# Up projection: operands of two products and the weight tiles of one begin at many byte residues

## The chip, the core and the metric

One core of one Trainium2 chip. The metric is device microseconds of one execution; the kernel before has a median of 1459.01 us in 3 runs (1456.24 to 1460.63). TensorE (PE) multiplies, with the weight load as a stream of its own (PEld), VectorE (DVE), ScalarE (ACT) and GpSimd (POOL) do the elementwise work, SyncE (SP) and ACT issue most DMAs.

## The reference

One layer of a hybrid decoder on 1024 tokens of width 1024: a mixing stage, then the gated MLP below, then an embedding gate and a final norm. All is fp32. The change is in the up projection of the MLP.

```python
def conv_glu_ffn(hn, w_up, conv_w, conv_b, w_down):
    u = hn @ w_up                       # (1024, 1024) @ (1024, 5632)
    up = jnp.pad(u, ((0, 0), (CONV_W - 1, 0), (0, 0)))
    uc = conv_b + conv_w[0] * up[:, 0:S_]
    for j in range(1, CONV_W):
        uc = uc + conv_w[j] * up[:, j:j + S_]
    gate, val = jnp.split(uc, 2, axis=-1)
    return (jax.nn.silu(gate) * val) @ w_down

    h = h + conv_glu_ffn(rmsnorm(h, norm_ffn_g[l]), ffn_up[l], ffn_conv_w[l], ffn_conv_b[l], ffn_down[l])
```

## The kernel before

**Precision.** Every fp32 product is made of three matmuls of type float32r: an operand is split into a part `hi` (ACT copies it to float32r) and a part `lo` (the rest, subtracted on DVE or POOL), and hi x hi, lo x hi and hi x lo are added in PSUM. In `mul` (L1388) part 0 is the weights' hi with the moving hi, part 1 the weights' hi with the moving lo, part 2 the weights' lo with the moving hi.

**Units.** The up projection (`phase_up`, L1494) runs in 22 units `f`. A unit takes 128 gate columns and 128 value columns of `ffn_up`, each loaded by SP as a 512 KB tile `raw` (four buffers, so two units). The 2 x 2 x 2 block product of a unit (gate and value columns; first and second 512 rows of the weights; first and second 512 tokens) is done with seven products instead of eight. Product n has a weight block made of sums of the raw blocks (`sums`, L1506, on DVE: `s7` is a11 + a21, `s6` adds a22, later a12) and a moving operand `TX["p1"]` to `TX["p7"]`, which is made once for all units. Each moving operand has four tiles of 128 x 512 for hi and four for lo. A product is 12 matmuls of 128 x 512 columns, a unit 84. The products run in this order, the first pairs interleaved matmul by matmul: p3 (of the unit before) with p1; p6 with p4 (of the unit before); p5 with p2; p7. Accumulators are PSUM tiles `bg` (gate half) and `bv` (value half), two of each.

**Weight tiles.** `split2` (L102) makes hi (`whi`, ACT) and lo (`wlo`) of a weight block. All seven blocks of a unit take their tiles from one ring of six buffers each, in the order 3, 1, 4, 6, 5, 2, 7; block 7's lo is made on DVE, the others' on POOL. The moving tiles of p1, p2 lie at the top of SBUF (`t16`), those of p5, p6 in tiles of the earlier stage, and those of p3, p7, p4 in a pool `ty` (`op_tiles`, L1407, filled by `op_split`). Every one of these tiles, moving or weight, begins 64 bytes past a multiple of 128 in its partition.

**Work around the products.** DVE adds the products' parts (L1564, L1572, L1576, L1585, L1587) and does the convolution (L1597, L1598) after a first pass on ACT (L1596); ACT applies silu (L1600), DVE multiplies the halves (L1605) and forms sums for the down projection (L1617 to L1620), which SP stores. L1587 reads `bv`, to which the next unit's p4 is added. In this stage the order on each engine is made by the framework's scheduler from the written order, the buffers and their releases.

Of the kernel before, what the change touches and what calls it, by code (L numbers as in the profile page):

```python
# [10 lines left out]
F32 = mybir.dt.float32  # L11
F32R = mybir.dt.float32r
U8 = mybir.dt.uint8
AF = mybir.ActivationFunctionType
ALU = mybir.AluOpType
# [3 lines left out]
P = 128  # L19
T = 1024  # L20
HT = 512
# [58 lines left out]
class Trunk:  # L80
# [1210 lines left out]
    def phase_out(self, hp, x0, emb):  # L1291


        nc = self.nc
        self.h = [hp.tile([P, T], F32, name=f"h{k}") for k in range(ND)]
        self.hd = [[self.zpool.tile([P, HT], F32, tag=f"hd{k}_{hf}", name=f"hd{k}_{hf}") for hf in (0, 1)] for k in range(ND)]
        todo = [lambda k=k: nc.scalar.dma_start(self.h[k], self.a["xT"][k]) for k in range(ND)]
        for _ in range(3):
            todo.pop(0)()
        acc = hp.tile([P, HT], F32, name="acc")  # L1300

        def rows(m, halves, hooks={}):
            w = self.load_w(self.a["w_out"][m])
            ps = self.dps.tile([P, T], F32, tag="dp", name=self.nm("dp"))
            self.dense([ps[:, :HT], ps[:, HT:]], w, self.O, (6, 7, 0, 1, 4, 2, 3, 5), halves, hooks)
            for g in halves:
                u = self.h[m][:, g * HT:(g + 1) * HT]
                nc.vector.tensor_tensor(u, u, ps[:, g * HT:(g + 1) * HT], ALU.add)
                last = nc.scalar.dma_start(self.hd[m][g], u)
            if todo:  # L1310
                with self.tc.issue_after(last.ins):
                    todo.pop(0)()

        for m in range(ND):
            rows(m, (0, 1) if m < 2 else (0,))
            self.sq_acc(acc, self.h[m][:, :HT], m == 0)
        r = {}

        def factor(i):
            if i == 0:  # L1320
                r[0] = self.rstd_sums(acc, 1.0 / 1024, EPS, self.mxp.tile([P, 4], F32, tag="mx", name=self.nm("ps_ss")))
            else:
                r[1] = self.rstd_spread(r[0], self.mxp.tile([P, HT], F32, tag="mx", name=self.nm("ps_ss")))

        with self.tc.manual_schedule(engines={mybir.EngineType.PE}):
            rows(2, (1,), {0: lambda: factor(0), 3: lambda: factor(1)})
        pb = r[1]
        x0.close()
        self.TX = {}
        for i, n in enumerate(("p1", "p2")):  # L1330
            self.TX[n] = [[self.tile16(8 * i + 2 * k + c, F32R) for c in (0, 1)] for k in range(4)]
        self.ped = [self.zpool.tile([P, T], F32, tag=f"pe{m}", name=f"pe{m}") for m in range(ND)]
        pwp = emb.enter_context(self.pool("pw"))
        px, pw = [], []
        parts = [(px, self.pxp, "pT", 0), (pw, pwp, "ple_proj", 0), (px, self.pxp, "pT", 1), (pw, pwp, "ple_proj", 1)]
        norm = self.ffn_norm(0, pb)
        for m in range(3, ND):
            rows(m, (1,))
            if m == 5:
                ins = self.raw_ins  # L1340
            for _ in range(2):
                next(norm, None)
            if parts:
                self.pe_load(pwp, *parts.pop(0))
        for m in range(ND):
            self.sq_acc(acc, self.h[m][:, HT:], m == 0)
        with self.tc.issue_after(ins):
            self.ffn_first()
        with self.tc.manual_schedule(engines={mybir.EngineType.PE}):
            for m in range(5):  # L1350
                self.embed(m, pw, px, self.dps.tile([P, T], F32, tag="dp", name=self.nm("dp")))
                if m in (1, 2):
                    factor(m - 1)
        self.pe_in = (pw, px)
        return r[1]
# [49 lines left out]
        return t  # L1405

    def op_tiles(self, pool, *names):  # L1407
        for n in names:
            self.TX[n] = [[pool.tile([P, HT], F32R, name=f"t{n}{p}{k}") for p in "hl"] for k in range(4)]

    def op_split(self, n, k, src):
        hi, lo = self.TX[n][k]
# [22 lines left out]
    def ffn_operands(self, hs, up, emb):  # L1435

        nc, h = self.nc, self.h
        V, G = nc.vector, nc.gpsimd
        split = self.op_split
        first = self.units[:2]  # L1440
        b0 = [t[:, :HT] for t in h]
        b1 = [t[:, HT:] for t in h]
        B11, B21, B12, B22 = b0[:4], b0[4:], b1[:4], b1[4:]
        us = {}

        def t4(k):
            V.scalar_tensor_tensor(B21[k], us[k], -1.0, B21[k], ALU.mult, ALU.subtract)

        for k in range(4):

            V.tensor_tensor(B11[k], B11[k], B12[k], ALU.subtract)
            us[k] = self.spool.tile([P, HT], F32, tag="sqt", name=self.nm("nu"), bufs=2)
            V.scalar_tensor_tensor(us[k], B11[k], -1.0, B22[k], ALU.mult, ALU.subtract)
            split("p6", k, us[k])
            if k:
                t4(k - 1)
        t4(3)
        for k in range(4):
            split("p5", k, B11[k])
        for d in first:  # L1460
            d["G"] = self.banks("g")
        with self.tc.manual_schedule(engines={mybir.EngineType.PE}):
            for m in (5, 6):
                self.embed(m, *self.pe_in, self.banks("v"))
            self.mul(*[(d["G"][:, :HT], d["w1"], self.TX["p1"], True) for d in first])
            self.embed(7, *self.pe_in, self.banks("v"))
        for d in first:
            self.keep_first(d)
        for d in first:
            d["w2"] = self.split2(d["raw"][:, HT:], V)  # L1470
        self.mul(*[(d["G"][:, :HT], d["w2"], self.TX["p2"], False) for d in first])
        for k in range(4):
            V.tensor_tensor(B12[k], B22[k], B12[k], ALU.subtract)
        emb.close()
        pool = up.enter_context(self.pool("ty"))
        self.op_tiles(pool, "p3", "p7", "p4")
        for n, B in (("p7", B12), ("p3", B22)):
            for k in range(4):
                split(n, k, B[k])

        def last_operand(after):
            with self.tc.issue_after(after):
                for k in range(4):
                    split("p4", k, B21[k])
            hs.close()
            self.cv = up.enter_context(self.pool("cv", side="right"))

        self.last_operand = last_operand

# [4 lines left out]
    def phase_up(self):  # L1494
        nc, par, ep, TX = self.nc, self.par, self.ep, self.TX
        V, G = nc.vector, nc.gpsimd
# [19 lines left out]
        def w(d, n):  # L1516
            if n == "3":
                V.tensor_tensor(d["s"]["3"], d["s"]["3"], d["s"]["2"], ALU.add)
            return self.split2(d["s"][n], V if n in "7" else G)

        def unit(d, prev):
            f = d["f"]
# [3 lines left out]
            ws = {}  # L1526
# [7 lines left out]
                sums(d)  # L1534
            for n in "652" if new else "65":
                ws[n] = w(d, n)
            ws["7"] = w(d, "7")
            def first():
                jobs = []
                if prev:  # L1540
                    jobs.append((prev["G"][:, HT:], ws["3"], TX["p3"], False))
                if new:
                    d["G"] = self.banks("g")
                    jobs.append((d["G"][:, :HT], ws["1"], TX["p1"], True))
                if jobs:
                    self.mul(*jobs)
# [79 lines left out]
        for d in self.units:  # L1626
            unit(d, prev)
            prev = d
        ws = {n: w(prev, n) for n in "34"}
# [310 lines left out]
```

## Time and profile before

| | |
|---|---|
| median of 3 runs | 1459.01 us (1456.24 to 1460.63) |
| span of the profiled execution, first to last instruction | 1457.3 us |
| mean granted TensorE clock | 0.994 |
| instructions | 20344 |
| up projection's matmuls of seven products (L1395) | 1848, starting at 718.4 to 1140.7 us |

The page gives no time of the profiled execution beside its span. Lines of the profile read "line, engine, operation, output<-inputs, shapes, count | busy us, mean ns of one | idle us before, and what ended it". In a timeline the first two numbers are start and duration in us. Matmuls are pipelined: a matmul lasts 0.39 us in the records, while the next one starts earlier, so the pace is read from starts.

### The profile page before, as it was taken

The page shows a single profiled execution, that of the slowest core. Times are in us where ns is not written, and L with a number is a line of the kernel's source. Part 1 is how long each engine was busy: PE and PEld are TensorE (multiplying, and loading weights), DVE is VectorE, ACT ScalarE, POOL GpSimd, SP SyncE. Part 2 cuts the span into 40 slices and gives each one's busy share as a digit, 9 for nine tenths or more (in the row PEclk, how much of TensorE's full clock was granted, in tenths as well). Part 3 has the DMA queues.
Part 4 walks back from the last instruction along what each step waited for, and adds up shares of the span by engine and source line. Part 5 has one row for each costly group of instructions (what it writes and reads, how often), then busy time and mean ns, then how long its engine had stood idle before and what let it go on. Part 6 is the DMA issues. An engine that isn't in the chain of part 4 may idle for free.

```text
span 1457.3 us, 20344 instructions
## 1 busy us (share of the span) xinstructions
PE 1428.6 (98%) x7480; PEld 1176.0 (81%) x7480; DVE 1102.4 (76%) x1672; ACT 634.7 (44%) x1131; POOL 449.2 (31%) x364
## 2 busy tenths in 40 slices
PE   9999999999999999899999999999999999999996
PEld 7888887888877777787888888888888888888885
DVE  6567566684777689637798889888888799777685
ACT  6531343213434565335554434444444444455552
POOL 2332432323421132222145445444454000002342
PEclk9999999999999999999999999999999999999998
DMA  5223021240251220165323332333333883351443
GB/s 214 70 80 116 30 73 58 66 130 30 65 196 52 109 73 28 65 224 205 145 97 114 109 97 99 110 101 108 105 98 122 314 283 96 103 166 58 126 156 116
DMA packets 80019, 167.84 MB, mean 115 GB/s; under 512 B 20080, under 2 KB 22256, under 8 KB 79920
## 3 DMA queue, kind: packets, MB, share of 16 engines
q1 hardware_dynamic: 65568, 145.44, 30.4%
q10 hardware_dynamic: 13408, 17.57, 3.6%
q0 software_dynamic: 944, 3.54, 0.7%
q8 instruction: 59, 0.97, 0.3%
q14 instruction: 40, 0.33, 0.1%
HBM read 120.12 MB, written 46.40 MB: 114 GB/s over the span
## 4 chain that ended last, share of the span: by engine, by line
PE 86%; DVE 6%; issue 3%; ACT 2%; POOL 1%; DMA 1%; SPq 0%; DVEq 0%; ACTq 0%; POOLq 0%
PE bg L1395 16%; PE bv L1395 12%; PE dp L130 8%; PE dp L132 8%; PE dp L134 8%; PE bg L1713 7%; PE bv L1713 7%; PE hsc L1073 1%; PE bv L130 1%; PE bv L134 1%; PE bv L132 1%; PE bg L130 1%; PE bg L134 1%; PE bg L132 1%; PE swq L1230 1%
## 5 line engine op out<-in xcount | busy, mean ns | idle before, releaser
L130 PE MATMUL dp<-xh,whi 128*128 128x512 f32 x544 | 197.7, 408 | 1.6 <-ACT xh L375 1.6
L132 PE MATMUL dp<-xl,whi 128*128 128x512 f32 x544 | 188.5, 392 | 0.3 <-DVE xl L376 0.3
L134 PE MATMUL dp<-xh,wlo 128*128 128x512 f32 x544 | 188.6, 392 | 0.0
L108 POOL TENSOR_TENSOR wlo<-wraw,whi 128x512 fp32r<-128x512 f32 x63 | 90.8, 1445 | 223.7 <-ACT whi L106 205.2
L108 POOL TENSOR_TENSOR wlo<-raw,whi 128x512 fp32r<-128x512 f32 x84 | 135.8, 1635 | 75.5 <-ACT whi L106 75.5
L1395 PE MATMUL bg<-t,whi 128*128 128x512 f32 x352 | 132.5, 389 | 0.6 <-DVE ct L1598 0.6
L106 ACT CAST whi<-wraw 128x512 fp32r<-128x512 f32 x120 | 72.5, 618 | 129.2 <-PE dp L132 86.8
L130 PEld LDWEIGHTS dp<-xh,whi 128*128 128x128 f32 x544 | 101.7, 189 | 24.0 <-issue 3.3
L134 PEld LDWEIGHTS dp<-xh,wlo 128*128 128x128 f32 x544 | 102.3, 188 | 22.4 <-issue 0.5
L132 PEld LDWEIGHTS dp<-xl,whi 128*128 128x128 f32 x544 | 102.5, 189 | 20.3 <-DVE xl L376 0.6
L108 POOL TENSOR_TENSOR wlo<-s,whi 128x512 fp32r<-128x512 f32 x44 | 66.5, 1511 | 161.2 <-ACT whi L106 161.2
L1713 PE MATMUL bg<-t,whi 128*128 128x512 f32 x308 | 94.9, 389 | 0.0
L1713 PE MATMUL bv<-t,whi 128*128 128x512 f32 x308 | 94.8, 389 | 0.0
L106 ACT CAST whi<-raw 128x512 fp32r<-128x512 f32 x88 | 52.7, 619 | 91.4 <-issue 48.5
L106 ACT CAST whi<-s 128x512 fp32r<-128x512 f32 x66 | 39.0, 621 | 122.0 <-PE bg L1395 113.4
L175 POOL TENSOR_TENSOR rst<-rst,mhalf 128x4 f32<-128x4 f32 (+1 forms) x9 | 10.2, 1132 | 223.7 <-DVE rst L173 223.7
L1395 PEld LDWEIGHTS bg<-t,whi 128*128 128x128 f32 x352 | 66.0, 188 | 14.7 <-ACT whi L106 1.0
L108 DVE TENSOR_TENSOR wlo<-wraw,whi 128x512 fp32r<-128x512 f32 x57 | 48.8, 855 | 38.1 <-ACT whi L106 33.7
L1709 ACT CAST t<-t 128x512 fp32r<-128x512 f32 x77 | 47.8, 622 | 47.9 <-PE bv L1713 35.4
L1713 PEld LDWEIGHTS bv<-t,whi 128*128 128x128 f32 x308 | 57.8, 188 | 12.0
L1713 PEld LDWEIGHTS bg<-t,whi 128*128 128x128 f32 x308 | 57.7, 188 | 12.0
L1395 PE MATMUL bg<-t,wlo 128*128 128x512 f32 x176 | 67.2, 389 | 0.0
(426 smaller groups left out, 3613.9 us busy)
## 6 DMA issues: line engine op xcount, KB each, us to landing
raw<-in_ffn_up_dram SPq DMA_DIRECT2D x44, 512.0 KB, 3.7
wraw<-in_w_in_dram SPq DMA_DIRECT2D x29, 512.0 KB, 3.8
z<-zst SPq DMA_DIRECT2D x18, 512.0 KB, 3.0
gb<-ct SPq DMA_DIRECT2D x33, 256.0 KB, 2.3
t<-gb SPq DMA_DIRECT2D x33, 256.0 KB, 2.9
t<-gt SPq DMA_DIRECT2D x33, 256.0 KB, 2.7
zl<-z SPq DMA_DIRECT2D x16, 512.0 KB, 4.5
wraw<-in_ple_gate_dram SPq DMA_DIRECT2D x16, 512.0 KB, 3.6
```

The source lines that it names most:

```text
L106: nc.scalar.copy(hi, src)
L108: eng.tensor_tensor(lo, src, hi.bitcast(F32), ALU.subtract)
L130: nc.tensor.matmul(ps[hf], wh, xh[hf], start=first, stop=False)
L132: nc.tensor.matmul(ps[hf], wh, xl[hf], start=False, stop=False)
L134: nc.tensor.matmul(ps[hf], wl, xh[hf], start=False, stop=last)
L175: nc.gpsimd.tensor_tensor(r2[:, :n], r[:, :n], self.mhalf[:, :n], ALU.pow)
L1073: nc.tensor.matmul(sc[:, c, :], ks[:, c * P:(c + 1) * P], view(qt, c * P, [2 * n, 64 // n], [HT + n, 2], [1, n]), start=True, stop=True)
L1230: nc.tensor.matmul(pq[h][:, b:b + w], d["q"][hs, qb * P:nk], d["k"][hs, b:b + w], start=True, stop=True)
L1395: nc.tensor.matmul(ps, w[part == 2][:, s], X[k][part == 1], start=start and k == part == 0, stop=k == 3 and part == 2, skip_group_check=no ...
L1709: nc.scalar.copy(xh, x)
L1713: nc.tensor.matmul(ps[m], wt[part == 2][:, m * P:(m + 1) * P], (xh, xl)[part == 1], start=k == part == 0, stop=k == NK - 1 and part == 2)
```

## The change

```diff
-        acc = hp.tile([P, HT], F32, name="acc")
+        acc = self.pxp.tile([P, HT], F32, name="acc")
...
     def op_tiles(self, pool, *names):
+
+        def tile(n, p, k):
+            if n == "p3":
+                return pool.tile([P, HT], F32R, name=f"t{n}{p}{k}")
+            o = 2 * (2 * k + (p == "l")) + (n == "p4")
+            return pool.tile([P, HT + 16], F32R, name=f"t{n}{p}{k}")[:, o:o + HT]
+
         for n in names:
-            self.TX[n] = [[pool.tile([P, HT], F32R, name=f"t{n}{p}{k}") for p in "hl"] for k in range(4)]
+            self.TX[n] = [[tile(n, p, k) for p in "hl"] for k in range(4)]
+
+    def split_offset(self, src, eng, o):
+        nc = self.nc
+        hi, lo = (self.dg.tile([P, HT + 16], F32R, tag=n, name=self.nm(n), bufs=2)[:, o:o + HT] for n in ("dh", "dl"))
+        nc.scalar.copy(hi, src)
+        eng.tensor_tensor(lo, src, hi.bitcast(F32), ALU.subtract)
+        return hi, lo
...
             hs.close()
             self.cv = up.enter_context(self.pool("cv", side="right"))
+            self.dg = up.enter_context(self.pool("dg"))
...
-            ws["7"] = w(d, "7")
+            ws["7"] = self.split_offset(d["s"]["7"], V, 3 * f % 16) if f > 2 else w(d, "7")
```

**Residues.** The tiles of p7 and p4 become 64 bytes longer, and the operand begins `o` floats into its tile. In the built program the moving tiles then begin at these bytes past a multiple of 128: p7 hi 64, 80, 96, 112, lo 8, 24, 40, 56; p4 hi 68, 84, 100, 116, lo 12, 28, 44, 60. From unit 3 on the weight tiles of "7" begin 4 x (3f mod 16) bytes past 64 or 0, by the buffer. All other operands of matmuls stay 64 past a multiple of 128.

**Buffers.** From unit 3 on the tiles of "7" come from two buffers of their own (`dh`, `dl`, in a new pool), and the ring of six serves six blocks a unit. `acc`, the sum of squares of the norm before, moves to the pool of the embedding's operands, and with it the tiles of h by 2048 bytes, which makes room for the new pool.

**Order.** On PE and POOL the instructions stand in the same order as before. On DVE and ACT the order changes. DVE, in the middle of the stage, from the addition to the value half of the unit before to the product of the halves; `s_1506` and `s_1530` are sums for the next unit and the one after, and before, `s_1530` stands five rows behind this piece, after the next L1564. Before:

```order
L1576 TENSOR_TENSOR bv_7980<-bv_7980,e_7972 128x512
L1597 SCALAR_TENSOR_TENSOR ct_8152<-bv_7980,ncw,ct_8152 128x1023
L1598 SCALAR_TENSOR_TENSOR ct_8152<-bv_7980,ncw,ct_8152 128x1022
L1585 TENSOR_TENSOR x_8194<-e_8116,bg_8091 128x512
L1605 TENSOR_TENSOR ct_8119<-ct_8119,ct_8152 128x1024
L1518 TENSOR_TENSOR s_1506_8228<-s_1506_8228,raw_8209 128x512
L1618 TENSOR_TENSOR ct_7975<-ct_8119,ct_7975 128x512
L1587 TENSOR_TENSOR bv_8124<-x_8194,bv_8124 128x512
```

And the same stretch with the change:

```order
L1591 TENSOR_TENSOR bv_7983<-bv_7983,e_7975 128x512
L1533 TENSOR_TENSOR s_1506_8231<-s_1506_8231,raw_8212 128x512
L1612 SCALAR_TENSOR_TENSOR ct_8155<-bv_7983,ncw,ct_8155 128x1023
L1525 TENSOR_TENSOR s_1530_8373<-raw_8356,raw_8358 128x512
L1613 SCALAR_TENSOR_TENSOR ct_8155<-bv_7983,ncw,ct_8155 128x1022
L1600 TENSOR_TENSOR x_8197<-e_8119,bg_8094 128x512
L1620 TENSOR_TENSOR ct_8122<-ct_8122,ct_8155 128x1024
L1527 TENSOR_TENSOR s_1531_8375<-s_1530_8373,raw_8358 128x512
L1633 TENSOR_TENSOR ct_7978<-ct_8122,ct_7978 128x512
L1602 TENSOR_TENSOR bv_8127<-x_8197,bv_8127 128x512
```

The sum with a12 (L1518, now L1533) moved ahead of the convolution, and the two sums s7 and s6 of the unit after next (L1525, L1527) now stand ahead of the addition that reads `bv` (L1587, now L1602).

ACT in the same place, from the gate half's first convolution pass on. Before:

```order
L1596 ACTIVATE ct_8119<-bg_7947,par 128x1024
L106 CAST whi_8218<-raw_8209 128x512
L106 CAST whi_8222<-raw_8055 128x512
L1600 ACTIVATE ct_8119<-ct_8119 128x1024
L1596 ACTIVATE ct_8152<-bv_7980,par,ncw 128x1024
L106 CAST whi_8231<-s_1506_8228 128x512
L106 CAST whi_8235<-raw_8211 128x512
L106 CAST whi_8239<-raw_8209 128x512
L106 CAST whi_8243<-s_1505_8226 128x512
```

And with the change:

```order
L1611 ACTIVATE ct_8122<-bg_7950,par 128x1024
L106 CAST whi_8225<-raw_8058 128x512
L1615 ACTIVATE ct_8122<-ct_8122 128x1024
L106 CAST whi_8234<-s_1506_8231 128x512
L1611 ACTIVATE ct_8155<-bv_7983,par,ncw 128x1024
L106 CAST whi_8238<-raw_8214 128x512
L106 CAST whi_8242<-raw_8212 128x512
L1421 CAST dh_8390<-s_1530_8373 128x512
```

The cast of block 1 (first in the old piece) now stands earlier, ahead of this piece; that of "6" moved ahead of the value half's pass; and the cast of "7" is that of a unit later (`s_1530` for `s_1505`).

## The prediction

> **What bounds the kernel now.** I read the page's totals and chain first, then the busy time by stage for the up projection, then single instructions of one of its units. The totals and the first row of the chain:
>
> ```profile
> PE 1428.6 (98%) x7480; PEld 1176.0 (81%) x7480; DVE 1102.4 (76%) x1672; ACT 634.7 (44%) x1131; POOL 449.2 (31%) x364
> PE 86%; DVE 6%; issue 3%; ACT 2%; POOL 1%; DMA 1%; SPq 0%; DVEq 0%; ACTq 0%; POOLq 0%
> ```
>
> TensorE is the bound, but 98% is an average over stages, so here is busy time in three stretches of the up projection (columns: sum, then PE, PEld, DVE, ACT, POOL with counts, granted clock, DMA share, GB/s):
>
> ```profile
> 780.00:820.00 40.00, 40.00 (x178) 33.11 (x177) 35.54 (x36) 17.26 (x24) 20.33 (x13) 1.00 0.34 112
> 900.00:940.00 40.00, 40.00 (x178) 33.14 (x177) 34.87 (x37) 17.34 (x24) 20.42 (x14) 1.00 0.31 99
> 1060.00:1100.00 40.00, 40.00 (x178) 33.14 (x177) 35.59 (x36) 15.84 (x22) 20.75 (x14) 1.00 0.33 106
> ```
>
> PE is busy all of each stretch at granted clock 1.00. DVE stands at 35.5 of 40 (89%): second in line, and what decides if its order gets worse. A busy PE says nothing yet of its pace, so the starts (start us, us):
>
> ```profile
> 904.24 0.39 PE L1395 MATMUL bv<-tp7h,whi 128*128 128x512 f32 x1
> 906.96 0.39 PE L1395 MATMUL bg<-tp3h,whi 128*128 128x512 f32 x1
> 912.40 0.39 PE L1395 MATMUL bv<-tp6h,whi 128*128 128x512 f32 x1
> 931.44 0.39 PE L1395 MATMUL bv<-tp6h,whi 128*128 128x512 f32 x1
> ```
>
> From 904.24 to 906.96 lie the 12 matmuls of p7, from 906.96 to 912.40 the 24 of p3 and p1: 2.72/12 = 5.44/24 = 0.2267 us each. One unit (84 matmuls) repeats after 931.44 - 912.40 = 19.04 us, which is 84 x 0.2267 again: no stall is left in a steady unit. The time of this stage is matmuls x 0.2267, whatever DVE, ACT and POOL do, as long as each is in time. So two questions decide: does the 0.2267 depend on where an operand begins, and is everybody still in time?
>
> **The change part by part.**
>
> *The pace of the matmuls.*
>
> ```profile
> L1395 PE MATMUL bv<-tp4h,whi 128*128 128x512 f32 x88 | 34.2, 389 | 0.0
> L1395 PE MATMUL bv<-tp4l,whi 128*128 128x512 f32 x88 | 34.2, 389 | 0.0
> L1395 PE MATMUL bv<-tp7h,whi 128*128 128x512 f32 x88 | 34.2, 389 | 0.0
> L1395 PEld LDWEIGHTS bv<-tp4h,whi 128*128 128x128 f32 x88 | 16.5, 188 | 3.4
> ```
>
> Each of p4 and p7 has three such groups of 88 (h with whi, l with whi, h with wlo), 264 matmuls; together 528, or 528 x 0.2267 = 119.7 us of PE time. Number and order of all matmuls stay. Of the 528, p4's 264 and the 88 with tp7l begin off a multiple of 16 bytes (352); the other 176 move by multiples of 16. In 228 of p7 (19 units x 12) the weights move too, off a multiple of 16 in 14 of the 19 units.
>
> Before, every operand of these begins at the same residue, so no row shows this price; I bound it by the nearest rows. For weights these are two plain fp32 products: in L668 the weights begin 64 past a multiple of 128, in L779 (columns of `par`: byte 8320 + 4 x 494) 56 past, so 8 past a multiple of 16. For the moving side, L1253 reads 128 contiguous columns, while L1073 reads the same number in strides that jump through `qt`.
>
> ```profile
> L668 PEld LDWEIGHTS bon<-prod,cst 128*128 128x128 f32 x8 | 1.5, 188 | 1.1 <-issue 0.7 <-ACT whi L106 0.2
> L779 PEld LDWEIGHTS pg<-sg,par 128*128 128x128 f32 x8 | 1.2, 191 | 0.0
> 90.66 1.88 PE L668 MATMUL bon<-prod,cst 128*128 128x512 f32 x4
> 218.17 1.02 PE L779 MATMUL pg<-sg,par 128*128 128x512 f32 x2
> L1253 PE MATMUL swt<-cst,lg 128*128 128x128 f32 x144 | 20.2, 281 | 1.6 <-ACT ob L1267 1.0 <-DVE zst L495 0.7
> L1073 PE MATMUL hsc<-qt,ks 128*128 128x128 f32 x224 | 32.3, 289 | 5.8 <-DVE qt L1078 4.6 <-ACT ks L1063 0.7 <-DVE hS L1054 0.3
> ```
>
> A load of the odd weights takes 191 against 188 ns, and either fits under the 227 ns of a matmul: nothing. The moving side shows 289 against 281, 8 ns more for scattered reading; 528 x 8 ns = 4.2 us is the upper end that I keep. The lower end: four L668 matmuls last 1.88 us with a tail of 0.59, so they start 0.43 us apart, and half of that, 0.215, is what 512 columns would take at just twice the plain fp32 pace. The 0.2267 is 0.012 above it. Were this surplus a matter of all operands sharing one residue and vanished, 528 x 0.012 = 6.3 us would go. I take 0, nearest to the weight rows, which alone differ in the residue and in nothing else of note.
>
> The Trainium skill, "Advanced Engine Details and Errata", section "SBUF Cachelines", speaks against the change: SBUF is read in 16-byte lines, and going to a new line costs. An operand off a multiple of 16 touches 129 lines for 128. By that, as an estimate, 352 x 227/128 = 0.6 us would be added; the strided row (+8 ns) agrees in direction, and the sum stays under what can be measured.
>
> *The order on DVE and ACT.* The split of "7" leaves the ring of six whi/wlo buffers. Before, seven splits a unit went round six buffers; now six do, and each has exactly a unit. Matmul order is unchanged, POOL keeps its order, but DVE now forms the sums (s7, s6) for the unit after next, behind the value half's first convolution step. Rows of before, unit n with its first matmul at 906.96:
>
> ```profile
> 906.81 1.78 DVE L1518 TENSOR_TENSOR s<-s,raw 128x512 f32<-128x512 f32 x1
> 910.20 0.68 DVE L1587 TENSOR_TENSOR bv<-x,bv 128x512 f32<-128x512 f32 x1
> 912.37 0.70 DVE L1564 TENSOR_TENSOR bg<-bg,v 128x512 f32<-128x512 f32 x1 [1.48 <-PE bg L1395]
> 912.62 0.39 PE L1395 MATMUL bv<-tp4h,whi 128*128 128x512 f32 x1
> 913.50 1.21 ACT L1596 ACTIVATE ct<-bg,par 128x1024 f32<-128x1024 f32 x1
> 913.70 1.66 DVE L1510 TENSOR_TENSOR s<-raw,raw 128x512 f32<-128x512 f32 x1
> 915.39 0.69 DVE L1512 TENSOR_TENSOR s<-s,raw 128x512 f32<-128x512 f32 x1
> 917.40 1.14 ACT L106 CAST whi<-raw 128x512 fp32r<-128x512 f32 x2 [2.69 <-issue]
> 918.10 2.56 POOL L108 TENSOR_TENSOR wlo<-raw,whi 128x512 fp32r<-128x512 f32 x2 [3.29 <-ACT whi L106]
> 919.16 1.06 ACT L1600 ACTIVATE ct<-ct 128x1024 f32<-128x1024 f32 x1 [0.62 <-DVE ct L1598]
> 922.87 1.28 DVE L1598 SCALAR_TENSOR_TENSOR ct<-bv,ncw,ct 128x1022 f32<-128x1022 f32 x1
> 924.67 1.26 DVE L1605 TENSOR_TENSOR ct<-ct,ct 128x1024 f32<-128x1024 f32 x1
> raw<-in_ffn_up_dram SPq DMA_DIRECT2D x44, 512.0 KB, 3.7
> ```
>
> The tight place is L1587: it must have read bv before the next p4 matmul adds to it. It ends at 910.88, p4 starts at 912.62: 1.74 us to spare, on a DVE that is never far ahead. Now the new order from the same rows. ACT takes "4" alone at 917.40 (0.62), POOL its lo half at 918.1 (1.3, half of the 2.56): done 919.4. Only then is the second weight buffer of unit n free for unit n+2, and its DMA lands 3.7 later, 923.1. DVE, with nothing now between the two steps of the gate half, is through them by 917.2 (ACT's pass ends at 914.7, two steps of 1.2), and with v and bv by 919.2. ACT runs its silu from 918.0 to 919.1, the cast of "6" to 919.7 and the value half's pass to 920.9, POOL the lo half of "6" to 921.0. For that DVE waits, adds a12 (to 921.7) and does one convolution step (to 922.9). So s7 (the former L1510) starts at 923.2, held 0.3 us by the DMA. Then 0.7 (s7), 1.2 (second step), 0.6 (x), 1.26 (ct x ct), 1.3 (s6, partly beside POOL), 0.7 (t5), 0.7 (L1587): done 929.7. The next p4 starts at 912.62 + 19.04 = 931.66: 2.0 us to spare, as before. DVE sums that run beside POOL take 1.66 to 1.78 instead of 0.69 (rows L1510, L1518 against L1512); were all of s7 and t5 so, 2.0 more, and the room would be just used up. All weights are split at least as early as before, since each waits for the release of its own predecessor, 13.6 us ahead of use (19.04 less the 5.44 of a pair of products). Sum of this part: 0, with 2 us of cover per unit.
>
> *The rest.* The casts of p4, p7 and "7" have the same shapes: 0. `acc` moves from the pool of h to that of the embedding, and h by 2 KB, so the loads of h wait for the release of other tiles of the mixing stage: 0, and what it may shift is left to D below.
>
> Sum: span 1457.3 + 0. The median of the three runs, 1459.01, lies 1.7 above the span (the page gives no other time of that execution), so the forecast is 1459.0.
>
> **The rivals.**
>
> *A, PE gets faster.* One residue for all operands is what costs the 0.012. For: the surplus is there. Against: it is the same in every product, at every time, whatever else reads SBUF. It gives 1459.0 - 6.3 = 1452.7. The Trainium skill, "TensorE: Matmul & The Clock Gate", section "Wait — 56ns, not 53.3ns?", gives 215.7 ns for back-to-back matmuls of 512 columns at full clock, and this trace has 226.7 at clock 1.00, so it does not agree; by its number 528 x 11 ns = 5.8 us could go.
>
> *B, a new wait (slower).* s7 now hangs on a DMA that started 3.7 us before, with L1587 behind it in DVE's queue and p4 behind that. Once the landing takes over 5.7 us, or over 3.7 with every sum slowed by POOL, PE stalls once a unit. At 0.4 us (a landing of 4.1 to 4.5 with slowed sums) x 18 units: +7 us, 1466. For: DVE at 89%. Against: the freed order has DVE beside POOL less often than before.
>
> *C, off-line reads cost.* 8 ns per matmul as in L1073: +4.2, 1463.2. Were such operands read at the plain fp32 pace (0.43), 352 x 0.20 = 70 us would come on top; no row hints at it.
>
> *D, something small outside the steady units moves* (the loads of h, the first units): within 5 us either way.
>
> **How the numbers follow.** A measurement of this kernel can tell about 0.3% (4.4 us) from no change. Forecast 0.68, A 0.08, B 0.11, C 0.09 (0.04 of it at +4.2 or less, still "same"), D 0.04, half on each side. Faster: 0.08 + 0.02 = 0.10. Same: 0.68 + 0.04 = 0.72. Slower: 0.11 + 0.05 + 0.02 = 0.18. Range: from 4 below the forecast, half way to A, to B's 1466; it takes in C's 4.2 and leaves out A, C's far end and D, 0.17 in all.
>
> **What would show it.** Right: groups of tp4 and tp7 at 389 ns and 12 matmuls in 2.72 us; the new dh/dl loads at 188; PE 40.00 of 40 in each stretch; s7 waiting a few tenths for a DMA and no PE wait on bv. A shows as p4 and p7 under 0.2267 per matmul and p3, p5, p6 at it; C as the same two above it, most where the start is odd. B shows as PE idle before p4, once a unit, released by DVE, with s7 behind a late DMA. Any of these, or a change in a stage other than the up projection, would make this wrong.

## The result, and the profile after

The changed kernel takes 1466.8 us (median of 4 runs, 1465.96 to 1467.56) against 1459.82 of the kernel before beside it (4 runs): ratio 1.0051, 95% interval 1.0036 to 1.0067. It is slower, where no change was forecast, and lies 0.8 us above the range. The profiled execution spans 1465.8 us, 8.5 more than before.

Totals and first row of the chain of waits, after:

```profile
PE 1434.6 (98%) x7480; PEld 1176.4 (80%) x7480; DVE 1055.2 (72%) x1672; ACT 630.7 (43%) x1131; POOL 417.7 (28%) x364
...
PE 86%; DVE 5%; issue 3%; ACT 2%; POOL 2%; DMA 1%; SPq 0%; DVEq 0%; ACTq 0%; POOLq 0%
```

TensorE is the bound as before, at the same share. DVE is busy 47 us less and POOL 32 less; the sum with a12, for one, takes 0.74 us on the average where it took 1.68. The prediction had DVE's sums run beside POOL less often, which fits, and it is worth nothing while PE is the bound. The same three stretches of the up projection as before the change, with columns as there:

```profile
780.00:820.00 40.00, 40.00 (x175) 32.77 (x175) 28.47 (x35) 15.39 (x22) 15.45 (x12) 0.99 0.28 94
900.00:940.00 40.00, 40.00 (x176) 32.73 (x175) 28.88 (x35) 16.53 (x24) 16.83 (x14) 1.00 0.29 100
1060.00:1100.00 40.00, 40.00 (x177) 32.81 (x176) 28.94 (x35) 16.46 (x23) 16.73 (x13) 1.00 0.31 104
```

PE is still busy 40.00 of 40: nothing waits in a steady unit. But it starts 175 to 177 matmuls where it started 178. A longer stretch shows it better (before, then after):

```profile
800.00:1100.00 300.00, 300.00 (x1325) 248.43 (x1324) 266.03 (x269) 124.27 (x173) 149.35 (x96) 1.00 0.32 103
```

```profile
800.00:1100.00 300.00, 300.00 (x1312) 245.96 (x1311) 221.29 (x265) 121.40 (x173) 120.90 (x94) 1.00 0.30 103
```

Thirteen matmuls fewer at 0.2267 us are 2.9 us lost in 300 us at full clock, with no idle time: the pace itself is worse. One steady unit of after says where (starts of p7, then of p3):

```profile
909.80 0.39 PE L1395 MATMUL bv<-tp7h,dh 128*128 128x512 f32 x1
...
912.65 0.40 PE L1395 MATMUL bg<-tp3h,whi 128*128 128x512 f32 x1
```

Its 12 matmuls of p7 take 2.85 us instead of 2.72. In the groups, p7 shows 395 ns for 389, and its weight loads 188 ns as before:

```profile
L1395 PE MATMUL bv<-tp7h,dl 128*128 128x512 f32 x76 | 30.0, 395 | 0.0
L1395 PE MATMUL bv<-tp7l,dh 128*128 128x512 f32 x76 | 30.0, 395 | 0.0
...
L1395 PEld LDWEIGHTS bv<-tp7h,dl 128*128 128x128 f32 x76 | 14.3, 188 | 3.4
```

The other loss is one place near the beginning. PE's waits in the up projection, and the chain of work through the longest of them (start, us, what):

```profile
PE bg L1395 <- DVE x L1600: 2.6, 2, 2.3
```

```profile
769.62 3.38 DMA raw<-in_ffn_up_dram
...
773.09 1.37 DVE s L1525
774.45 1.13 DVE ct L1620
775.59 0.61 DVE x L1600
776.20 0.14 issue
776.33 7.31 PE bg L1395 x24
```

Read upward from PE: p3 may add to `bg` only after x has read it, x stands in DVE's queue behind s7 of unit 4, and s7 waits for its weights' DMA. Two windows, of the stall and of what follows it:

```profile
773.70:776.30 2.60, 0.35 (x2) 0.00 (x0) 2.60 (x4) 1.14 (x2) 0.80 (x2) 1.00 0.00 0
776.30:780.40 4.10, 4.07 (x11) 3.23 (x12) 4.10 (x6) 0.00 (x0) 0.68 (x1) 0.58 0.70 260
```

PE idles 2.25 us and then runs 4.1 us at a granted clock of 0.58: seven matmuls start 426 to 427 ns apart.

From the starts of all 1848 matmuls, the up projection takes 430.71 us after and 422.25 before, +8.46:

| part | us |
|---|---|
| p4 and p7 at 232.4 ns a matmul instead of 226.67, and the products next to them | +4.2 |
| the stall at 773.7 (2.67 us from start to start instead of 0.23) | +2.4 |
| the half clock behind it (11 matmuls in 4.19 us instead of 2.49) | +1.7 |
| a second wait for x at 1124.0 (0.75 us and a slow start) | +0.6 |
| a stall of before at 756.7 that is 0.5 shorter | -0.5 |

The rest of the span takes 1035.1 us in both.

### The profile page after: what moved, and what is told of

The parts are those of the page before. It is cut to its first block, busy times and chain, and to the rows that moved or that the text cites. A ratio compares the mean times of both kernels' runs of the same rounds, so it can differ in the third digit from the quotient of the medians.

```text
span 1465.8 us, 20369 instructions
## 1 busy us (share of the span) xinstructions
PE 1434.6 (98%) x7480; PEld 1176.4 (80%) x7480; DVE 1055.2 (72%) x1672; ACT 630.7 (43%) x1131; POOL 417.7 (28%) x364
## 4 chain that ended last, share of the span: by engine, by line
PE 86%; DVE 5%; issue 3%; ACT 2%; POOL 2%; DMA 1%; SPq 0%; DVEq 0%; ACTq 0%; POOLq 0%
PE bg L1395 16%; PE bv L1395 12%; PE dp L130 8%; PE dp L134 8%; PE dp L132 8%; PE bg L1728 7%; PE bv L1728 7%; PE hsc L1073 2%; PE bv L130 1%; PE bv L134 1%; PE bv L132 1%; PE bg L130 1%; PE bg L134 1%; PE bg L132 1%; PE swq L1230 1%
## 5 line engine op out<-in xcount | busy, mean ns | idle before, releaser
L108 POOL TENSOR_TENSOR wlo<-raw,whi 128x512 fp32r<-128x512 f32 x84 | 111.7, 1338 | 116.6 <-ACT whi L106 116.6
L1395 PE MATMUL bg<-t,whi 128*128 128x512 f32 x352 | 133.5, 392 | 0.1
L108 POOL TENSOR_TENSOR wlo<-s,whi 128x512 fp32r<-128x512 f32 x44 | 59.4, 1350 | 155.3 <-ACT whi L106 120.5
L1395 PEld LDWEIGHTS bg<-t,whi 128*128 128x128 f32 x352 | 66.3, 189 | 14.5 <-ACT whi L106 0.5
L106 ACT CAST whi<-s 128x512 fp32r<-128x512 f32 x47 | 28.8, 615 | 105.2 <-PE bg L1395 96.5
L1395 PE MATMUL bg<-t,wlo 128*128 128x512 f32 x176 | 67.5, 391 | 0.0
```

Source lines behind the costliest of these rows:

```text
L106: nc.scalar.copy(hi, src)
L108: eng.tensor_tensor(lo, src, hi.bitcast(F32), ALU.subtract)
L1395: nc.tensor.matmul(ps, w[part == 2][:, s], X[k][part == 1], start=start and k == part == 0, stop=k == 3 and part == 2, skip_group_check=no ...
```

## The experiments

A number is used below that no group of the profile gives: the **pace loss**, the sum over the 1848 matmuls of L1395 of the distance to the next start less 226.67 ns, where a distance counts for at most 245 (most of what is longer is a stall or the half clock, and is told apart). The matmuls that run slowly just behind a stall are in it. It is 0.07 us before and 4.5 after.

### Order and residues apart

`e1_order` is after with all offsets gone: same buffers, same order on DVE, ACT and POOL, all operands at 64.

```
-            o = 2 * (2 * k + (p == "l")) + (n == "p4")
-            return pool.tile([P, HT + 16], F32R, name=f"t{n}{p}{k}")[:, o:o + HT]
+            return pool.tile([P, HT], F32R, name=f"t{n}{p}{k}")
...
-        hi, lo = (self.dg.tile([P, HT + 16], F32R, tag=n, name=self.nm(n), bufs=2)[:, o:o + HT] for n in ("dh", "dl"))
+        hi, lo = (self.dg.tile([P, HT], F32R, tag=n, name=self.nm(n), bufs=2) for n in ("dh", "dl"))
```

> After's buffers and order (split of 7 in its own pair of buffers from unit 3 on, acc moved), but every operand back at 64 past a multiple of 128. If the loss has two parts, one from the order (a stall near 774 us in which DVE holds s behind a raw DMA and x behind s, then a stretch of half clock) and one from the residues, this keeps only the first: stall of 2 to 3 us near 774, clock 0.5 for 3 us behind it, every matmul of a steady unit at 226.67 ns; up projection 4 us longer than before, about 1463.8. Rival, the stall too comes of the offsets (slower DVE or ACT work on shifted tiles): no stall, 1459.8. Second rival, the whole loss is order: 1466.8, and the pace stays above 226.67 in p4 and p7.

Measured: 1462.98 us, ratio 1.0035 (1.0023 to 1.0048). The wait is there without any offset:

```profile
PE bg L1395 <- DVE x L1600: 2.8, 2, 2.4
```

and the pace is that of before (x1325 in the long window, pace loss 0.3):

```profile
800.00:1100.00 300.00, 300.00 (x1325) 248.26 (x1325) 225.46 (x269) 120.78 (x173) 122.68 (x95) 1.00 0.30 103
```

In this execution the clock stayed at 1.00 behind a stall as long as after's:

```profile
773.40:777.50 4.10, 4.08 (x18) 3.39 (x19) 4.10 (x6) 0.00 (x0) 0.67 (x1) 1.00 0.69 256
```

It took 1459.59, the shortest of the five. e5 and f5 below have the stall without the half clock too; e3 and f7 have both. So the half clock is a sequel of the stall that comes in some executions; the last section says in which.

`e2_moving` leaves "7" in the ring of six (`ws["7"] = w(d, "7")`) and shifts only the moving tiles.

> Only the moving operands of p4 and p7 are shifted; 7 is split through the ring of six as before. Two-part theory: no stall near 774, but p7 and p4 still 5 to 6 ns above 226.67 per matmul and the products behind p7 settling back: 4.5 us over before, 1464.3. Rival, the pace is lost only where weights and moving operands are shifted together: p7 and p4 at 227 to 228, 1460. Rival, all is order: 1459.8.

Measured: 1462.26, ratio 1.0033 (1.0021 to 1.0046). No wait for x, up projection 426.12 us, pace loss 4.5, in p7 6.2 ns and in p4 5.8 ns a matmul:

```profile
800.00:1100.00 300.00, 300.00 (x1311) 245.87 (x1310) 264.62 (x267) 123.84 (x172) 147.88 (x95) 1.00 0.31 103
```

`e3_weights` shifts only the weights of 7 (after's `split_offset`, moving tiles as in e1).

> Only the weights of 7 are shifted, by 0 to 60 bytes from unit 3 on; all moving operands at 64. If a matmul's pace depends on the moving side alone: the order's stall of 4 us and pace 226.67 everywhere, 1463.8. If any operand off the common residue breaks the pace: p7 of 19 units at 232 (1.3 us) and 1 us in the products behind it, 1466.

Measured: 1462.38, ratio 1.0035 (1.0022 to 1.0047); the stall and the half clock of after, and a pace loss of 1.7 us, 0.4 of it behind the stalls, the rest in p7 and in the dozen matmuls behind it. The time alone can't be told from that of e1; the starts can. So there are two losses, each of which comes without the other (e1, e2), of about the same size, and the second comes when the moving side alone or the weights alone are shifted. The two ratios add up to more than after's (1.0068 for 1.0051), within their intervals.

### Which residue

`e4_all80`, `e6_mv0` and `e7_96_68` shift the moving tiles of p7 and p4 by one amount each (in whole 16-byte steps but for p4's 68), with weights and order of before. `e5_both80` moves p7 and its weights to 80. All pad the tiles to 2176 bytes, for instance:

```
-            o = 2 * (2 * k + (p == "l")) + (n == "p4")
-            return pool.tile([P, HT + 16], F32R, name=f"t{n}{p}{k}")[:, o:o + HT]
+            o = 4
+            return pool.tile([P, HT + 32], F32R, name=f"t{n}{p}{k}")[:, o:o + HT]
```

> Moving operands of p4 and p7, high and low parts alike, all at one other residue, 80 past a multiple of 128 (whole 16-byte steps); weights and order as before. If it is the mixing of residues within a product that loses the pace: p7 at 226.67 after its first few matmuls, p4 and p6, which alternate 80 and 64, at 232 (264 x 2 x 5.5 ns = 2.9 us at most): 1461 to 1463. If every residue but 64 costs: p7 and p4 both 5.7 ns up, 1462.9 to 1464. If only starts off a multiple of 16 cost: 226.67 everywhere, 1459.8.

> Moving operands of p7 and (from unit 3 on) its weights all at 80 past a multiple of 128; p4 and all else at 64. After's order, so its stall near 774 is there (about 4 us with the half clock). If what counts is the distance between the weights' start and the moving start: p7 at 226.67 ns per matmul with 3 to 8 disturbed ones where the residue changes, pace loss under 1 us, 1460 to 1461. If 64 itself is special: p7 at 231 as with the moving side alone at 80, pace loss 1.2 us.

> Moving operands of p4 and p7 all at 0 past a multiple of 128, 64 bytes from the weights; order of before. If the pace repeats with 64 bytes: 226.67 everywhere and the time of before. If with 128: p7 above 226.67 in a fixed pattern of three, as at 80 (234, 234, 225), and p4 with p6 near 232; 3 to 4.5 us over before.

> Moving operands of p7 all at 96 (32 bytes off), of p4 all at 68 (4 bytes off); weights and order of before. If the loss grows with the distance between the residues: p7 up by more than the 4.3 ns of 80, p4 with p6 by under 1 ns. If any other residue costs the same: p7 4 to 6 ns, p4 with p6 5 ns on the average, 4 us over before. If it takes a crossing of a 32-byte or 64-byte boundary, p7 at 96 is free and p4 is not.

Measured: pace loss 4.4, 2.0, 4.2 and 7.1 us; ratios 1.0030, 1.0040, 1.0023 and 1.0042. Whole 16-byte steps cost about as much as e2's mixture, e5 missed both of its expectations, equal residues for p7 and its weights did not help, and 64 bytes apart was no better than 16. Read like this, 64 looked special. Three kernels with every operand moved test that. all96 moves both ends of memory up by 32 bytes, with a small tile at the bottom and another size of `edge` at the top:

```
-            self.cpool = e(tc.tile_pool(name="const", bufs=1))
+            self.cpool = e(tc.tile_pool(name="const", bufs=1)); self.cpool.tile([P, 8], F32, name="pad")
...
-            e(self.pool("edge", side="right")).tile([P, 40], F32, name="edge")
+            e(self.pool("edge", side="right")).tile([P, 32], F32, name="edge")
```

all0 and all32 make room by letting two small tiles of the norm share one place (`r2 = r`). all0 moves the lower end down by 64 bytes and the upper end up by 64, all32 by 32 and 96.

> The kernel before, with every tile on chip moved by 32 bytes, so that all operands of all stages begin at 96 past a multiple of 128 where they began at 64. If what counts is that operands share a residue: 226.67 ns per matmul in the up projection and the time of before within 2 us. If 64 itself is the good place: 230 ns or more everywhere, 6 us or more over before in the up projection alone (1848 matmuls by 3.5 ns) and 20 us in the whole kernel.

> As all96, with all operands at 0 past a multiple of 128 (two small tiles of the norms become one, to make room). Sharing counts: 226.67 and the time of before. 64 special: 230 or more, 20 us over. If 64 and 0 are alike because both are multiples of 64, this is as before and the runs at 96 and 32 are not.

> As all96, with all operands at 32 past a multiple of 128. Sharing counts: 226.67 and the time of before. 64 special, or multiples of 64: 230 or more, 20 us over.

Measured: all96 1456.51, ratio 1.0001 (0.9992 to 1.0011); all0 1468.99, 1.0082 (1.0067 to 1.0097); all32 1468.89, 1.0085. The long window of all96, then of all0:

```profile
800.00:1100.00 300.00, 300.00 (x1326) 248.39 (x1325) 265.06 (x268) 123.81 (x173) 148.92 (x95) 1.00 0.31 104
```

```profile
800.00:1100.00 300.00, 300.00 (x1314) 246.10 (x1313) 264.95 (x268) 123.86 (x172) 147.39 (x95) 1.00 0.31 102
```

64 is not special: 96 runs as well. What is wrong with all0 and all32 is seen product by product: p7 and p4 with p6 keep 226.67, but p3 with p1 and p5 with p2 run at 234.4 and 225.6 ns in turn. p1 and p2 are the products whose moving tiles (`t`) lie at the upper end of memory, with all weights at the lower; and the two shifts of each kernel (64 and 64 bytes, 32 and 96) put them 128 bytes apart modulo 256, though alike modulo 128. Before, the tile of every operand of this stage begins at 1856 modulo 2048. The down projection, whose moving tiles lie above too, loses more: in all0 all of its 924 matmuls are 128 apart and start every 233.3 ns on the average instead of 226.7, 6.2 us in all. Busy time of all0's last stage, then that of before:

```profile
1145.00:1460.00 315.00, 310.59 (x1365) 250.92 (x1363) 243.13 (x375) 146.23 (x247) 46.11 (x34) 1.00 0.46 150
```

```profile
1145.00:1460.00 315.00, 301.16 (x1351) 249.13 (x1349) 241.40 (x376) 144.48 (x245) 48.19 (x35) 0.98 0.47 152
```

So 128 was the wrong unit, and the tiles of 2176 bytes (17 x 128) had spoilt the four kernels above: every other tile lay 128 off. In e5 that can be read off. From unit 3 on its weights lie at 80 and at 208 modulo 256 in turn, its high parts at 80, its low parts at 208. In units where 4 of p7's 12 matmuls have weights and moving operand apart, p7 loses 49 to 50 ns (10 units); where 8 of 12 have, 66 to 80 ns, mostly 73 (9 units).

### What must agree, and modulo what

With spacers ahead of the tiles in place of padding, each operand lies at a known place modulo 2048. f1 (p7 128 past all others, p4 32 past), f2 (32 and 64) and f3 (p7's low parts 256 past, p4 512) differ in the numbers of one line, and in f1 p4 is laid out ahead of p7. All three move `acc` as the change does, which f3 shows to be free. The line as f1 has it:

```
+        T = {}
         for n in names:
+            for p in "hl":
+                if z := {'p4h': 8, 'p7h': 24}.get(n + p):
+                    pool.tile([P, z], F32, name="z" + n + p)
+                for k in range(4):
+                    T[p, k] = pool.tile([P, HT], F32R, name=f"t{n}{p}{k}")
```

> Modulo 2048, all operands at one place but p7's moving ones, all at 128 past it, and p4's, all at 32 past it (p4 alternates with p6, which is at 0). Order and weights of before. If a start must agree with the start before it: p7 at 226.67 but for a few matmuls at its borders (0.3 us or less in 22 units), p4 with p6 3 to 6 ns up (1.6 to 3.2 us). If a start must agree with the weights': p7 up by 4 ns or more in all its matmuls too.

> As f1 with p7 at 32 past the common place and p4 at 64. Start to start: p7 at 226.67 but for its borders, p4 with p6 3 to 6 ns up. Start to weights: p7 up by 3 ns or more.

> Shifts by multiples of 256 only: p7's low parts 256 past its high ones (they alternate), p4's all 512 past. Unit of 256: 226.67 in every product, the time of before. A unit of 512 or more: p7 up by 3 to 7 ns; of 1024: p4 with p6 up too.

Measured: f1 1461.58, ratio 1.0031; f2 1462.17, 1.0035; f3 1457.46, ratio 1.0000 (0.9991 to 1.0010). Long window of f1, then of f3:

```profile
800.00:1100.00 300.00, 300.00 (x1310) 245.68 (x1310) 264.87 (x267) 123.31 (x172) 146.19 (x95) 1.00 0.31 102
```

```profile
800.00:1100.00 300.00, 300.00 (x1325) 248.40 (x1324) 265.04 (x268) 124.00 (x173) 148.91 (x95) 1.00 0.31 104
```

f3 has operands at three places and loses nothing: the unit is 256. In f1 all moving tiles of p7 lie at one place and all its weights at one other; within the product no moving start differs from the one before it, and still each of its matmuls but the first two takes 229 or 237.6 ns in turn, to the end of the product. The first matmul of p7 and the first behind it, in f1:

```profile
904.97 0.40 PE L1395 MATMUL bv<-tp7h,whi 128*128 128x512 f32 x1
...
907.76 0.39 PE L1395 MATMUL bg<-tp3h,whi 128*128 128x512 f32 x1
```

These 12 take 2.79 us, 2.72 before. So it isn't the change from one moving operand to the next that costs, it is the moving start against the weights'.

The same for the weights: f5 puts a spacer of 128 bytes at the head of the pool of dh and dl, f7 one of 256, f6 sets p7's moving tiles and dh and dl 128 past all others together.

> After's order and buffers; all moving operands at one place, the weights of 7 (from unit 3 on) all at 128 past the place of the other weights modulo 2048. Its stall near 772 stays (3 us, with the half clock 5). If weights must agree with the weights before them: p7 at 226.67 but for its borders. If weights must agree with the moving side: p7 up by 4 ns or more throughout. If the weights' start counts only modulo 128: 226.67 throughout, borders too.

> After's order and buffers, with the weights of 7 (from unit 3 on) 256 past all others; all moving operands at one place. If 256 is the unit for weights as for the moving side: 226.67 throughout, only the stalls of the order, time of e1_order (ratio 1.0035) within 1 us. If the weights' unit is larger: p7 at 230 or more, as with 128.

> After's order and buffers, with p7's moving operands and (from unit 3 on) its weights both 128 past the place of all others modulo 2048; the stalls of the order stay. If a matmul's moving operand and its weights must agree with each other modulo 256: from unit 3 on p7 at 226.67 but for 1 to 3 matmuls where it begins, and p3 and p1 behind it for as many; pace loss in all under 0.6 us, against the 1.5 to 2.3 of the runs that shifted one side by 128. If each must agree with the operands of the neighbouring products: p7 at 230 or more throughout, 1.5 us or more.

Measured: f5 1463.16, ratio 1.0045 (1.0030 to 1.0060), p7 at 233 ns from unit 3 on, pace loss 2.3. f7 1461.82, ratio 1.0031 (1.0019 to 1.0042), pace loss 0.4, p7 at 226.67. Long window of f5, then of f7:

```profile
800.00:1100.00 300.00, 300.00 (x1317) 247.15 (x1316) 223.07 (x267) 121.63 (x174) 123.13 (x96) 1.00 0.30 102
```

```profile
800.00:1100.00 300.00, 300.00 (x1325) 248.40 (x1324) 223.16 (x267) 122.59 (x175) 122.58 (x96) 1.00 0.30 103
```

f6: 1461.35, ratio 1.0024 (1.0015 to 1.0034), no more than the order's loss alone (1.0035 in e1, 1.0031 in f7), as expected if the two starts must agree. Its interval just reaches that of f5, and its pace could not be read from its trace, so that a pair off all others but in agreement runs at 226.67 rests on this time only.

All runs in one table, with the matmuls of the up projection whose moving start and weights' start differ modulo 256, by the addresses of their tiles:

| run | pairs apart, of 1848 | pace loss, us | ns per pair |
|---|---|---|---|
| before, all96, f3 | 0 | 0.07, 0.07, 0.04 | |
| e1, e8, f7, e9 (below) | 0 | 0.3, 0.2, 0.4, 1.7 | |
| f6 | 36 | not read | |
| e5 | 148 | 2.0 | 14 |
| e3, f5 | 228 | 1.7, 2.3 | 8, 10 |
| e2 | 484 | 4.5 | 9 |
| after | 520 | 4.5 | 9 |
| all0, all32, e6, e4, f1, f2, e7 | 528 | 3.6, 3.6, 4.2, 4.4, 4.6, 5.9, 7.1 | 7 to 14 |

No pair apart, no loss (what e1, e8, f7 and e9 have lies in the slow starts behind their stalls, of which e9 has 18). In every run with pairs apart there is a loss, 7 to 14 ns for each pair; that includes its neighbours' share and, in e3, e5 and f5, 0.2 to 0.4 us of slow starts behind the stalls. How the price depends on the distance is not settled: in e3 one of the 19 units, with weights 28 and 156 past the moving start, lost nothing.

### The order

`e8_hold` and `e9_holdall` are e1 with unit 4's sums, or those of every unit from 2 on, held until unit f - 2 has made its last addition. The line of e8:

```
-            with self.tc.issue_after(self.units[0]["x"]) if f == 2 else ExitStack():
+            with self.tc.issue_after(self.units[f - 2]["x"]) if f in (2, 4) else ExitStack():
```

> As e1_order (after's order and buffers, all operands at 64), but the sums of unit 4 are issued behind unit 2's last addition, so that x no longer stands behind s and its DMA in DVE's queue. If that queue is the whole of the order's loss: no PE wait near 771, up projection 422.5 us, the time of before within 1 us. Rival, the late raw DMA holds up something else (the weights of unit 4): the stall moves on by a unit and 2 us or more stay.

> As e8_hold, with the sums of every unit from 2 on issued behind the last addition of the unit two ahead, so that no sum for later stands ahead of x in DVE's queue, as before the change; all operands at 64. If those sums are the whole of the order's loss: no PE wait from 760 to 1140 but the 1 us near 756 that before has too, up projection 422.5 us. Rival, the sum that makes the weights of 3 (which waits for POOL) holds x as well: a stall of 1 to 2 us stays in one of the first units.

Measured: e8 1459.66, ratio 1.0014 (1.0005 to 1.0023); e9 1472.62, ratio 1.0108 (1.0091 to 1.0125). PE's waits for x, e8 and then e9 (us in total, times, longest):

```profile
PE bg L1395 <- DVE x L1600: 1.7, 2, 1.3
```

```profile
PE bg L1395 <- DVE x L1600: 9.4, 18, 2.1
```

Without s7 of unit 4 ahead of x the stall near 771 is gone, and 1.0035 becomes 1.0014. But a unit on, at 791, PE waits 1.3 us for x again, now behind the sum that makes the weights of 3 (L1533), which waits for POOL. DVE in e8:

```profile
788.72 0.69 DVE L1533 TENSOR_TENSOR s<-s,raw 128x512 f32<-128x512 f32 x1 [1.86 <-POOL wlo L108]
789.33 1.28 DVE L1612 SCALAR_TENSOR_TENSOR ct<-bv,ncw,ct 128x1023 f32<-128x1023 f32 x1
790.52 0.68 DVE L1525 TENSOR_TENSOR s<-raw,raw 128x512 f32<-128x512 f32 x1
791.12 1.28 DVE L1613 SCALAR_TENSOR_TENSOR ct<-bv,ncw,ct 128x1022 f32<-128x1022 f32 x1
792.32 0.68 DVE L1600 TENSOR_TENSOR x<-e,bg 128x512 f32<-128x512 f32 x1
```

In e9 it is ct times ct (L1620) that comes to stand ahead of x, PE waits for x 18 times, and the up projection takes 438.9 us. Neither kernel reached the time of before, which was the main expectation of both, and the rivals came true only in part. In e8 the stall did move on by a unit, but behind a sum that waits for POOL and not behind a late weight DMA; in e9 one wait in an early unit was foreseen. What both show is that x's place in DVE's queue makes the wait, and that holding a sum changes who stands ahead of x. Which order has no stall with these buffers was not found. No run beats the kernel before.

## Why the prediction was wrong, point by point

**The bound: right.** PE is busy 40.00 of 40 in each steady stretch, so a loss of pace is a loss of time.

**The pace: the step that failed.** "I take 0, nearest to the weight rows" should have been +4.2. The two weight rows compared the duration of a load, 191 against 188 ns. After, the loads of p7's weights still take 188, and the loss stands in the distance between the starts of the matmuls. Those products also start matmuls 430 ns apart, so they could hide what a stream at 227 shows. The upper end kept from the strided row, 8 ns x 528 = 4.2 us, met the size (measured 4.2 to 4.5, 9 ns for each of 520 pairs), and so the price of rival C came, but by luck: its mechanism was scattered or off-line reads, and what costs is two starts that disagree modulo 256. It also missed two details: p7's low parts, which begin off a multiple of 16, lose no more than its high parts (395 ns both), and products that were not moved lose with their neighbours.

**The rule of 16-byte lines** (the Trainium skill, "Advanced Engine Details and Errata", section "SBUF Cachelines"; 0.6 us by that estimate) doesn't explain it: f1 and f2 shift by whole lines and lose 6 to 7 ns a matmul in p7, as much as odd shifts.

**Rival A: refuted, with its sign turned.** Sharing one residue isn't what costs the 0.012 us above 0.215; it is what keeps the pace as low as 0.2267. Nothing here ran a product faster.

**The order in a steady unit: right in its times.** s7 was foreseen 16.2 us after p3's start, held 0.3 by the DMA; in the trace it starts at 928.83, 16.2 after p3's 912.65, held 0.22, and no PE wait follows. Rows of DVE, then the next p3 of PE:

```profile
928.83 0.69 DVE L1525 TENSOR_TENSOR s<-raw,raw 128x512 f32<-128x512 f32 x1 [0.22 <-DMA raw<-in_ffn_up_dram]
...
930.64 0.68 DVE L1600 TENSOR_TENSOR x<-e,bg 128x512 f32<-128x512 f32 x1
...
931.90 0.40 PE L1395 MATMUL bg<-tp3h,whi 128*128 128x512 f32 x1
```

**The order as a whole: failed.** "Sum of this part: 0, with 2 us of cover per unit" was worked out for one reader, L1587, and from one steady unit only. The tight place is x, which p3 waits for, and the listing of the change shows s7 ahead of x too. Before, in a steady unit, x ended at 924.75, 1.25 us ahead of p3:

```profile
924.07 0.68 DVE L1585 TENSOR_TENSOR x<-e,bg 128x512 f32<-128x512 f32 x1
...
926.00 0.39 PE L1395 MATMUL bg<-tp3h,whi 128*128 128x512 f32 x1
```

The prediction's own chain ends x at 925.7 (923.2 + 0.7 + 1.2 + 0.6), 0.3 us ahead of that p3, but it never compared the two. After, 0.4 to 0.8 us are left in each steady unit (0.58 in the rows above), so little that one late DMA is enough. Near 770 the DMA of unit 4's weights starts as it did before (769.62, before 769.50), but s7, which stood behind x there, now stands ahead of it and is held 1.49 us, not 0.3. Rival B had the mechanism (s7 on a DMA, with others behind it in DVE's queue), but not the place: it named L1587 and p4 in every unit, and it was x and p3, near 774 and, for a short wait, at 1124. The 1466 that it gave lies near the result by chance. That a stall of 2.3 us can cost 1.7 more through the clock stood nowhere.

**The rest (acc, h): right,** 1035.1 us in both.

Together: 4.2 of pace and 4.2 of order for 0 and 0. B and C, at 0.11 and 0.09, were priced as alternatives, and something like each came; the range took in either and not both.

## What to carry to other kernels

For a stream of matmuls, compare starts, not durations. Where it is like this one (float32r, 512 columns, weights of its own for each matmul), check the addresses of both operands of each matmul modulo 256, across pools and both ends of memory; here shifts of 64 or 128 bytes on one side were enough to break the agreement, and shifts of 256 were free. A steady unit says nothing of the first ones: work the chain out there too, with the DMA where it really starts, and ask of each instruction that waits for a DMA who stands behind it in its queue, and how much time each reader that PE waits for has to spare. Rivals with different causes can come together, and the range has to hold their sum.

## What the runs showed of the hardware

In this stage a float32r matmul of 512 columns with its own 128 x 128 weights starts every 226.67 ns if moving operand and weights begin at the same place modulo 256 bytes (before, all96, f3, f7). If they don't, the distances lie between 223 and 242 ns with few exceptions, and a product averages 230 to 235 ns in a run; one unit of e3 lost nothing. Behind a stall or such a product it takes up to a dozen matmuls until the distance is 226.67 again. Weights are loaded while matmuls stream (PEld is busy 33 of 40 us beside PE's 40), and within a product of f1 or f5 the weights of one matmul and of the next lie at the same distance from the moving start; so the runs don't say whether the stream must agree with its own weights or with those that are loaded beside it. What in the memory has this period no run shows either. The Trainium skill, "SBUF — State Buffer", section "Who interferes with whom", gives PE one read port for moving operands and one for weights and calls them independent; f1 and f5, where it is the distance between the two starts that costs 6 ns a matmul, do not agree with reads that never affect each other.

The granted clock fell to half 2.6 to 3.8 us after PE had begun to wait for x in after, e3, f7 and e9, and it did not in e1, e5, f5 and e8. In each trace the changes of the granted clock lie whole multiples of 3.413 us apart. If PE's wait is laid on this grid of steps, the two groups part: 2.28, 2.29, 1.93 and 2.10 us of the wait lie in one step in after, e3, f7 and e9, and the clock halves at its end; in e1, e5, f5 and e8 the wait is split over two steps or short, and no step holds more than 1.25, 1.40, 1.23 and 1.31 us. So it depends on where the grid happens to lie whether the stall costs 1.7 us more. This is read from eight executions; no run moved the grid alone, and in earlier stages steps with 1.7 to 1.9 us of idleness came out either way, so no exact bound follows. The Trainium skill, "TensorE: Matmul & The Clock Gate", section "What's actually happening", gives the half clock after at least one idle window of about 3.4 us and calls the window free-running; the traces agree with the window and its free running, but here 1.93 us of idleness in a step were enough. Its 426.7 ns for 512 columns at half clock (section "Wait — 56ns, not 53.3ns?") agrees with the 426 to 427 ns measured.
